# A decoder trunk of two layers in FP32: a third unit of each mixer group by seven products, and two units' low parts summed by DMA

## The chip, the cores and the metric

The kernel runs on one NeuronCore of one Trainium2 chip. The time is the device time of one execution in microseconds; of several runs the median is taken. The engines are TensorE (PE), VectorE (DVE), ScalarE (ACT), GpSimd (POOL) and the queue of SyncE (SP), from which the loads are issued.

## The reference, cut to what matters

Two decoder layers on 256 tokens of width 2048 with FP32 data. Each has a self-attention of 12 heads (a sliding window of 128 in the first layer, one causal block of 256 in the second), 4 heads into 256 memory tokens, an output projection, a layer norm, and a channel mixer with a layer norm behind it:

```
h   = layer_norm(ALPHA * h + mix, g0, b0)
ffn = square(relu(h @ w_up[layer])) @ w_down[layer]      # 2048 -> 8192 -> 2048
h   = layer_norm(ALPHA * h + ffn, g1, b1)
```

The change is in the channel mixer. Everything else of the layers stays as it is.

## The kernel before

Every FP32 operand of a matmul is split into a high part (rounded to a shorter float, tile `whi` for weights) and a low part (what the rounding left, tile `wlo`). A product of two operands is three matmuls into one bank of PSUM: high by high, high by low, low by high (`mm3`, L269 to L273). The split of weights is `split` (L96): ACT writes the high part, DVE subtracts it from the loaded tile `raw` and writes the low part.

The mixer goes through 8192 hidden columns in four chunks of 2048. In a chunk, two up groups compute 1024 hidden columns each, and then two down groups add the chunk's part to 1024 output columns each. A group (`mlp_group`) sums over 2048 inputs in eight units; a unit is a pair of k-tiles of 128 by 1024 columns of weights, 1 MB, loaded by one DMA into one tile `raw`. The 256 tokens are two halves of 128, so a unit is a 2 x 2 by 2 x 2 block product, and there are two ways for it:

- an ordinary unit (`weights`) multiplies every block: 4 banks x 2 k-tiles x 3 matmuls. Its weights are two `whi`/`wlo` pairs of 1024 columns, h0 (B11, B22) and h1 (B12, B21).
- a fast unit takes seven products, by Winograd's form of Strassen's scheme. DVE makes sums of weight blocks in a second tile `t` (`fast_weights`) and sums of activation blocks (`fast_acts`, tiles `sums`, made once and used by all groups with the same activations). Its weights take four `whi`/`wlo` pairs. Three of the products go to banks `P5`, `P6`, `P7` and one to `P1`, which DVE and ACT add up after the last fast unit (`early`); the other three go straight to the group's own banks.

A fixed table, `UP` and `DOWN`, says in which order the units of a group come and how many (those with the lowest numbers) are fast. In both, units 0 and 1 are fast and stand third and fifth. Tiles come from pools with a fixed number of buffers: 7 `whi`, 7 `wlo`, 4 `raw` (shared by loads, `t` and the raw activation sums). An instruction that wants a buffer waits until its last reader is done. On each engine the order of the instructions is written when the kernel is built, by a list scheduler that takes the program's order as its priority.

An up group's result is squared, transposed on PE and split into the next activations `gT`. These transposes (`back`, `transposed`, L443) are put into the stream of the following group at the places of `UHOOKS`: pairs of position in the group and bank. The first use of the activation sums is handed over in the same way, as steps of a generator hung on such places.

In the last chunk of each layer the second down group, and in the second layer the first up group, are plain products (`aform`) and not mixer groups.

Of the kernel before, what the change touches and what calls it, by code (L numbers as in the profile page):

```python
# [9 lines left out]
F32R = mybir.dt.float32r  # L10
I32 = mybir.dt.int32
AF = mybir.ActivationFunctionType
ALU = mybir.AluOpType
AX = mybir.AxisListType

P = 128
# [14 lines left out]
SCALE = float(P) ** -0.5  # L31
SLOPES = [2.0 ** (-8.0 * (i + 1) / HEADS) for i in range(HEADS)]
FAR = -1e33
NRAW = 4
NHI = 7
NLG = 4
HOLD = 13
# [28 lines left out]
NWARM = 2  # L66
FILL = (10, 11, 12, 16)

UP = ((2, 3, 0, 4, 1, 5, 6, 7), 2)
DOWN = ((2, 3, 0, 4, 1, 5, 6, 7), 2)  # L70
UHOOKS = ((0, 3), (1, 0), (1, 2), (1, 3))
WTAIL = ((1, 2), (2, 0), (3, 1), (5, 2), (7, 1), (9, 2))


# [1 line left out]
def trunk(ctx: ExitStack, tc: tile.TileContext, a: dict, out: bass.AP):  # L76
    nc = tc.nc
# [3 lines left out]
    ap_ = ctx.enter_context(tc.tile_pool(name="act", bufs=1))  # L81
# [14 lines left out]
    def split(hi, lo, src):  # L96
        nc.scalar.copy(hi, src)  # L97
        nc.vector.tensor_tensor(lo, src, hi.bitcast(F32), ALU.subtract)  # L98
# [26 lines left out]
    def fast_acts(xs, units):  # L125

        parts = []
        for j in range(0, len(units), 2):  # L130
            n = len(units[j:j + 2])
            x = xs[j // 2][:, :2 * n]
            raw = wp.tile([P, 2, 8, P], F32, name="x_f", tag="raw", bufs=NRAW)
            f = raw[:, 0, :4 * n].rearrange("p (k t) c -> p k (t c)", t=2)
            nc.vector.tensor_tensor(f, x[:, :, 0].bitcast(F32), x[:, :, 1].bitcast(F32), ALU.add)
            a11, a21 = f[:, 0:2 * n:2, :P], f[:, 0:2 * n:2, P:]
            a12, a22 = f[:, 1:2 * n:2, :P], f[:, 1:2 * n:2, P:]
            s = raw[:, 1, :4 * n].rearrange("p (u q) c -> p u q c", q=4)
            nc.vector.scalar_tensor_tensor(s[:, :, 0], a21, -1.0, a22, op0=ALU.mult, op1=ALU.subtract)
            nc.vector.scalar_tensor_tensor(s[:, :, 1], s[:, :, 0], -1.0, a11, op0=ALU.mult, op1=ALU.subtract)  # L140
            nc.vector.tensor_tensor(s[:, :, 2], a11, a21, ALU.subtract)
            nc.vector.tensor_tensor(s[:, :, 3], a12, s[:, :, 1], ALU.subtract)
            parts += [s[:, u] for u in range(n)]
        yield
        for (hi, lo), s in zip(units, parts):
            split(hi, lo, s)
        yield

    def sum_units(n, tags):
        units = []  # L150
        for tag in tags[:n]:
            if tag == "pts":
                units.append([ap_.tile([P, 4, P], F32R, name="sums", tag="pts", bufs=2) for _ in range(2)])
            else:
                t_ = ap_.tile([P, 2, 4, P], F32R, name="sums", tag=tag)
                units.append([t_[:, s] for s in range(2)])
        return units

    def weights(src, parts=1):


        raw = wp.tile([P, 2048], F32, name="raw", tag="raw", bufs=NRAW)
        n = 2048 // parts
        for c in range(0, 2048, n):
            nc.sync.dma_start(raw[:, c:c + n], src[:, c:c + n])
        halves = []
        n = min(n, 1024)
        for s in range(2):
            hi = wp.tile([P, 1024], F32R, name="whi", tag="whi", bufs=NHI)
            lo = wp.tile([P, 1024], F32R, name="wlo", tag="wlo", bufs=NHI)  # L170
            for c in range(0, 1024, n):
                split(hi[:, c:c + n], lo[:, c:c + n], raw[:, s * 1024 + c:s * 1024 + c + n])
            halves.append((hi, lo))
        return halves

# [79 lines left out]
    def mlp_group(src, xts, sums, hooks, early, order, nfast):  # L255

        ps = [ps_mm.tile([P, 512], F32, name="ps_g", tag="mm") for _ in range(4)]
        own = {}  # L260
        seen = {}
        last = {}

        fast = ("P1", 0, 1, "P5", "P7", "P6", 2)
        for u in order:
            for i in range(7 if u < nfast else 4):
                last[fast[i] if u < nfast else i] = (u, i)

        def mm3(bank, x, w, st, en):  # L269
            (xh, xl), (hi, lo) = x, w  # L270
            nc.tensor.matmul(bank, xh, hi, start=st, stop=False)  # L271
            nc.tensor.matmul(bank, xh, lo, start=False, stop=False)  # L272
            nc.tensor.matmul(bank, xl, hi, start=False, stop=en)  # L273

        def tok(k, t):
            return [xts[k // 4][:, k % 4, s, t * P:(t + 1) * P] for s in range(2)]

        left = nfast
        for pos, u in enumerate(order):
            k0, k1 = 2 * u, 2 * u + 1  # L280
            if u < nfast:
                for i in range(4):
                    hooks.get((pos, i), nothing)()
                if not own:
                    for nm in ("P1", "P5", "P6", "P7"):
                        own[nm] = ps_at.tile([P, 512], F32, name=nm, tag="at")
                w = fast_weights(src[u])
                sx = [[s[:, q] for s in sums[u]] for q in range(4)]
                prods = (("P1", tok(k0, 0), "B11"), (0, tok(k1, 0), "B21"), (1, sx[3], "B22"),
                         ("P5", sx[0], "T1"), ("P7", sx[2], "T3"), ("P6", sx[1], "T2"), (2, tok(k1, 1), "T4"))  # L290
                for i, (b, x, wn) in enumerate(prods):
                    mm3(own[b] if b in own else ps[b], x, w[wn], b not in seen, last[b] == (u, i))
                    seen[b] = True
                left -= 1
                if not left:
                    early(own)
                continue
            (h0, l0), (h1, l1) = weights(src[u])
            w = {"B11": (h0[:, :512], l0[:, :512]), "B22": (h0[:, 512:], l0[:, 512:]),
                 "B12": (h1[:, :512], l1[:, :512]), "B21": (h1[:, 512:], l1[:, 512:])}  # L300
            for b in range(4):
                hooks.get((pos, b), nothing)()
                t, n = b // 2, b % 2 + 1
                mm3(ps[b], tok(k0, t), w[f"B1{n}"], b not in seen, False)
                mm3(ps[b], tok(k1, t), w[f"B2{n}"], False, last[b] == (u, b))
                seen[b] = True
        return ps
# [289 lines left out]
    for l in range(LAYERS):  # L597
        more = l + 1 < LAYERS
        wq, wk, wv, wqm = (a[f"{n}{l}"] for n in ("wq", "wk", "wv", "wqm"))
        ps, _ = aform([wv[0, i] for i in range(4)], hT, hooks={6: lambda: next(mem["mk_rest"])})  # L600
        v = evict_v(ps, "v")
# [3 lines left out]
        for g in range(KVH):  # L605
            kt = ap_.tile([P, T], F32, name="kt", tag="kt", bufs=2)
            wform_sum(wk[g], hT, kt, pipe.hooks(*WHOOKS))
            for hd in range(g * GROUP, (g + 1) * GROUP):
                qt = new_q()
# [6 lines left out]
        for m in range(MH):  # L616
            qt = new_q()
# [5 lines left out]
        for nb in range(4):  # L623
            ps, fin = aform([a["wo"][l, nb, i] for i in range(4)], ot, hold=(0 if nb < 3 else 8 if more else HOLD),
                            hooks=pipe.tail() if nb == 0 else {})
# [5 lines left out]
        sum_h = None  # L631
        for c in range(FF // CH):
            gt = new_acts("og", "gT")
            todo = []
            sum_g = sum_units(DOWN[1], ("v", "mk"))
            for v_ in range(CH // 1024):

                hooks = dict(zip(UHOOKS, todo))
                us = [None] * 4
                if c == 0 and v_ == 0 and not more:  # L640
                    for nb in range(2):
                        ps, fin = aform([a["wup_s"][nb, i] for i in range(4)], hT, hold=(16 if nb == 0 else 0))
                        if nb == 0:
                            us[0] = relu2(ps[0])
                            fin()
                            us[2] = relu2(ps[1])
                        else:
                            us[1], us[3] = relu2(ps[0]), relu2(ps[1])
                else:
                    if sum_h is None:  # L650
                        sum_h = sum_units(UP[1], ("sum_h0", "sum_h1", "pts"))
                        steps = fast_acts(hT, sum_h)
                        hooks[0, 0] = hooks[1, 1] = lambda s=steps: next(s)
                    if v_ == 1:
                        steps = fast_acts(gt, sum_g)
                        hooks[5, 0] = hooks[6, 0] = lambda s=steps: next(s)
                    acc = []
                    ps = mlp_group(a["wup"][l, c * (CH // 1024) + v_], hT, sum_h, hooks, sums_up(acc), *UP)
                    for b in range(4):
                        nc.vector.tensor_tensor(acc[b], acc[b], ps[b], ALU.add)  # L660
                        nc.scalar.activation(acc[b], acc[b], AF.Relu)
                        nc.scalar.activation(acc[b], acc[b], AF.Square)
                    us = acc

                def back(b, v_=v_, us=us, gt=gt):
                    transposed(us[b], gt[2 * v_ + b % 2], b // 2, 0)
                todo = [lambda b=b, f=back: f(b) for b in (0, 1, 2, 3)]
# [80 lines left out]
```

## Time and profile before

| | |
|---|---|
| time, median of 3 runs | 2015.75 us (2015.15 to 2016.75) |
| the profiled execution: time | 2016.56 us |
| the profiled execution: span of the core | 2014.4 us |
| mean granted clock of TensorE | 0.997 of full speed |
| TensorE busy | 1994.2 us |
| VectorE busy | 1543.9 us |
| ScalarE busy | 1046.0 us |
| GpSimd busy | 1.2 us |
| moved by DMA | 391.63 MB, 194 GB/s over the span |

The span is one execution as the hardware profiler saw it; the time has some 2 us around it. Busy times say what an engine did, not whether anybody waited for it; matmuls are pipelined, so their records overlap, and the pace is the distance of their starts. Lines (L271) are those of the kernel's listing.

### The profile page before, as it was taken

Reading aid. Unit: us, or ns where it says so; the run is one execution under the profiler, and the core shown is the slowest. Engines: PE = TensorE matmul, PEld = TensorE weight load, DVE = VectorE, ACT = ScalarE, POOL = GpSimd, SP = SyncE. Lnnn points to the kernel's source line nnn. Section 1 sums busy time; section 2 is a strip of 40 time slices with the busy share of each in tenths; the row PEclk is TensorE's granted clock in tenths of the full one; section 3 lists DMA queues with packets and bytes.
Section 4 is the critical chain, followed back from the end, with each engine's and each line's share of the span. In section 5 each row is a group of like instructions: output and inputs, shape, how many; then the busy total and the mean of one; then the engine's idle time right before and its main releaser. Section 6 shows DMA issues by size and latency. Waiting matters only on the chain.

```text
span 2014.4 us, 23998 instructions
## 1 busy us (share of the span) xinstructions
PE 1994.2 (99%) x9326; PEld 1662.3 (83%) x9326; DVE 1543.9 (77%) x1961; ACT 1046.0 (52%) x1361; POOL 1.2 (0%) x8
## 2 busy tenths in 40 slices
PE   9999999999999999999999999999999999999997
PEld 7888888888888888888888888778888888888886
DVE  6566659988787888878785665688878887878885
ACT  6455534654564555466444554346455545654651
POOL 0000000000000000000000000000000000000000
PEclk9999999999999999999999999999999999999999
DMA  9644554555456555456654446445564555555651
GB/s 336 251 160 152 191 185 169 215 203 207 169 186 225 214 177 194 172 188 240 245 225 168 160 160 204 147 146 188 206 216 184 190 186 188 199 218 191 238 209 73
DMA packets 56273, 391.63 MB, mean 194 GB/s; under 512 B 6368, under 2 KB 6368, under 8 KB 9696
## 3 DMA queue, kind: packets, MB, share of 16 engines
q1 hardware_dynamic: 56160, 390.10, 53.7%
q8 instruction: 73, 1.20, 0.2%
q14 instruction: 40, 0.33, 0.0%
HBM read 387.98 MB, written 2.10 MB: 194 GB/s over the span
## 4 chain that ended last, share of the span: by engine, by line
PE 96%; DVE 3%; issue 0%; DMA 0%; ACT 0%; SPq 0%; DVEq 0%
PE ps_g L271 18%; PE ps_g L273 18%; PE ps_g L272 18%; PE ps_w L209 7%; PE ps_a L231 5%; PE ps_a L232 5%; PE ps_a L233 5%; PE ps_w L211 4%; PE P L271 3%; PE P L273 3%; PE P L272 3%; PE pt_h L443 2%; PE ps_m L553 1%; PE ps_m L554 1%; PE ps_m L555 1%; DVE h L436 1%
## 5 line engine op out<-in xcount | busy, mean ns | idle before, releaser
L98 DVE TENSOR_TENSOR wlo<-raw,whi 128x1024 fp32r<-128x1024 f32 (+1 forms) x706 | 818.1, 1174 | 329.7 <-ACT whi L97 325.2
L97 ACT CAST whi<-raw 128x1024 fp32r<-128x1024 f32 (+1 forms) x706 | 697.2, 1014 | 624.5 <-PE ps_g L273 349.7
L271 PE MATMUL ps_g<-whi,hT 128*128 128x512 f32 x780 | 306.7, 393 | 0.0
L273 PE MATMUL ps_g<-whi,hT 128*128 128x512 f32 x780 | 303.8, 390 | 0.0
L272 PE MATMUL ps_g<-wlo,hT 128*128 128x512 f32 x780 | 303.7, 389 | 0.0
L271 PE MATMUL ps_g<-whi,gT 128*128 128x512 f32 x728 | 286.4, 393 | 0.0
L273 PE MATMUL ps_g<-whi,gT 128*128 128x512 f32 x728 | 283.7, 390 | 0.0
L272 PE MATMUL ps_g<-wlo,gT 128*128 128x512 f32 x728 | 283.4, 389 | 0.0
L273 PEld LDWEIGHTS ps_g<-whi,hT 128*128 128x128 f32 x780 | 146.4, 188 | 30.8
L271 PEld LDWEIGHTS ps_g<-whi,hT 128*128 128x128 f32 x780 | 146.5, 188 | 29.4
L272 PEld LDWEIGHTS ps_g<-wlo,hT 128*128 128x128 f32 x780 | 146.6, 188 | 29.3
L273 PEld LDWEIGHTS ps_g<-whi,gT 128*128 128x128 f32 x728 | 136.7, 188 | 28.9
L97 ACT CAST whi<-t 128x1024 fp32r<-128x1024 f32 x116 | 122.0, 1052 | 72.5 <-PE ps_g L273 45.1
L272 PEld LDWEIGHTS ps_g<-wlo,gT 128*128 128x128 f32 x728 | 136.8, 188 | 27.3
L271 PEld LDWEIGHTS ps_g<-whi,gT 128*128 128x128 f32 x728 | 136.7, 188 | 27.2
L98 DVE TENSOR_TENSOR wlo<-t,whi 128x1024 fp32r<-128x1024 f32 x116 | 141.5, 1222 | 20.9 <-ACT whi L97 20.5
L209 PE MATMUL ps_w<-hT,whi 128*128 128x512 f32 x320 | 119.9, 414 | 0.0
L209 PE MATMUL ps_w<-xT,whi 128*128 128x512 f32 x320 | 119.9, 414 | 0.0
L231 PE MATMUL ps_a<-whi,ot 128*128 128x512 f32 x256 | 101.7, 397 | 0.0
L233 PE MATMUL ps_a<-whi,ot 128*128 128x512 f32 x256 | 99.8, 390 | 0.0
L232 PE MATMUL ps_a<-wlo,ot 128*128 128x512 f32 x256 | 99.7, 389 | 0.0
L211 PE MATMUL ps_w<-xT,wlo 128*128 128x256 f32 x320 | 89.9, 281 | 0.0
(170 smaller groups left out, 2832.0 us busy)
## 6 DMA issues: line engine op xcount, KB each, us to landing
raw<-in_wup_dram SPq DMA_DIRECT2D x120, 1024.0 KB, 4.8
raw<-in_wdn_dram SPq DMA_DIRECT2D x112, 1024.0 KB, 4.9
raw<-in_wo_dram SPq DMA_DIRECT2D x32, 1024.0 KB, 4.8
raw<-in_wq_dram SPq DMA_DIRECT2D x24, 1024.0 KB, 4.8
raw<-in_wdn_s_dram SPq DMA_DIRECT2D x16, 1024.0 KB, 4.8
raw<-in_wmk_dram SPq DMA_DIRECT2D x8, 1024.0 KB, 6.2
raw<-in_wv_dram SPq DMA_DIRECT2D x8, 1024.0 KB, 7.3
raw<-in_wk_dram SPq DMA_DIRECT2D x8, 1024.0 KB, 4.9
```

Of the source, the lines that this page charges most:

```text
L97: nc.scalar.copy(hi, src)
L98: nc.vector.tensor_tensor(lo, src, hi.bitcast(F32), ALU.subtract)
L209: nc.tensor.matmul(ps, hi[:, kk:kk + P], x.rearrange("p s t -> p (s t)"), start=(k == 0), stop=False)
L211: nc.tensor.matmul(ps[:, :T], lo[:, kk:kk + P], x[:, 0], start=False, stop=(k == KT - 1))
L231: nc.tensor.matmul(ps[t], xh, hi, start=st, stop=False)
L232: nc.tensor.matmul(ps[t], xh, lo, start=False, stop=False)
L233: nc.tensor.matmul(ps[t], xl, hi, start=False, stop=en)
L271: nc.tensor.matmul(bank, xh, hi, start=st, stop=False)
L272: nc.tensor.matmul(bank, xh, lo, start=False, stop=False)
L273: nc.tensor.matmul(bank, xl, hi, start=False, stop=en)
L436: nc.vector.scalar_tensor_tensor(ht[:, c], ht[:, c], mean, g, op0=ALU.subtract, op1=ALU.mult)
L443: nc.tensor.transpose(pt[:, k], src[:, k * P:(k + 1) * P], ident)
```

## The change

`UP` and `DOWN` now name three fast units, 0, 1 and 2, at the second, fourth and sixth place. The two ordinary units between them, 4 and 5, are listed in `SUMMED`: their low parts are no longer made by DVE. ACT writes the negated high part into `wlo`, a DMA issued from GpSimd adds the loaded weights onto it, and ACT writes the high part. The third unit of activation sums takes buffers of the tags `qt` and `pts`, in quarter tiles, and the splits of the activation sums are made in halves. There are five `raw` buffers. The hooks of the transposes stand earlier, the activation sums of the first layer are made ahead of the first group, and the scratch for GpSimd's DMA descriptors is twice as large.

```diff
-NRAW = 4
+NRAW = 5
...
-UP = ((2, 3, 0, 4, 1, 5, 6, 7), 2)
-DOWN = ((2, 3, 0, 4, 1, 5, 6, 7), 2)
-UHOOKS = ((0, 3), (1, 0), (1, 2), (1, 3))
+UP = ((3, 0, 4, 1, 5, 2, 6, 7), 3)
+DOWN = ((3, 0, 4, 1, 5, 2, 6, 7), 3)
+
+SUMMED = (4, 5)
+UHOOKS = ((0, 1), (0, 2), (0, 3), (1, 0))
...
         for (hi, lo), s in zip(units, parts):
-            split(hi, lo, s)
+            for q in range(2):
+                split(hi[q], lo[q], s[:, 2 * q:2 * q + 2])
...
             if tag == "pts":
-                units.append([ap_.tile([P, 4, P], F32R, name="sums", tag="pts", bufs=2) for _ in range(2)])
+                t_ = [ap_.tile([P, 4, P], F32R, name="sums", tag="pts", bufs=2) for _ in range(2)]
+                units.append([[t[:, :2], t[:, 2:]] for t in t_])
+            elif tag == "qt":
+                t_ = [ap_.tile([P, 2, P], F32R, name="sums", tag="qt", bufs=4) for _ in range(4)]
+                units.append([t_[:2], t_[2:]])
...
-            for c in range(0, 1024, n):
-                split(hi[:, c:c + n], lo[:, c:c + n], raw[:, s * 1024 + c:s * 1024 + c + n])
+            if summed:
+                src_s = raw[:, s * 1024:(s + 1) * 1024]
+                nc.scalar.activation(lo, src_s, AF.Copy, scale=-1.0)
+                nc.gpsimd.dma_start(lo, src_s, accum_op=ALU.add)
+                nc.scalar.copy(hi, src_s)
+            else:
+                for c in range(0, 1024, n):
+                    split(hi[:, c:c + n], lo[:, c:c + n], raw[:, s * 1024 + c:s * 1024 + c + n])
...
-            (h0, l0), (h1, l1) = weights(src[u])
+            (h0, l0), (h1, l1) = weights(src[u], 1, u in SUMMED)
...
-            sum_g = sum_units(DOWN[1], ("v", "mk"))
+            sum_g = sum_units(DOWN[1], ("v", "mk", "pts"))
...
-                        sum_h = sum_units(UP[1], ("sum_h0", "sum_h1", "pts"))
+                        sum_h = sum_units(UP[1], ("sum_h0", "sum_h1", "qt"))
                         steps = fast_acts(hT, sum_h)
-                        hooks[0, 0] = hooks[1, 1] = lambda s=steps: next(s)
+                        if more:
+                            list(steps)
+                        else:
+                            hooks[0, 0] = lambda s=steps: next(s)
+                            hooks[0, 2] = lambda s=steps, f=hooks[0, 2]: (f(), next(s))
...
-    nc = bacc.Bacc("TRN2", target_bir_lowering=False, num_devices=1, dynamic_dma_scratch_size=1024)
+    nc = bacc.Bacc("TRN2", target_bir_lowering=False, num_devices=1, dynamic_dma_scratch_size=2048)
```

## Rows read from the trace of the kernel before

**Rows 1.** The page: busy us (share of span) x instructions; the chain that ended last.

```profile
PE 1994.2 (99%) x9326; PEld 1662.3 (83%) x9326; DVE 1543.9 (77%) x1961; ACT 1046.0 (52%) x1361; POOL 1.2 (0%) x8
...
PE 96%; DVE 3%; issue 0%; DMA 0%; ACT 0%; SPq 0%; DVEq 0%
```

**Rows 2.** PE's waits, whole run: who waited for whom, total us, times, longest.

```profile
PE pt_h L443 <- DVE h L437: 4.2, 2, 2.2
PE ps_m L553 <- ACT whi L97: 2.0, 1, 2.0
```

**Rows 3.** Windows of both layers' mixers: busy us of each engine, clock, DMA.

```profile
core 0: us, PE busy (x) PEld busy (x) DVE busy (x) ACT busy (x) POOL busy (x), PEclk, DMA share, GB/s
...
330.30:1012.00 681.70, 681.70 (x3070) 564.51 (x3069) 564.49 (x630) 377.75 (x444) 0.00 (x0) 1.00 0.56 202
1360.00:1990.00 630.00, 630.00 (x2837) 521.64 (x2836) 512.81 (x574) 338.81 (x397) 0.00 (x0) 1.00 0.54 196
```

**Rows 4.** Groups by line: count, busy us, mean ns, idle before.

```profile
L271 PE MATMUL P<-whi,sums 128*128 128x512 f32 x174 | 67.7, 389 | 0.0
...
L660 DVE TENSOR_TENSOR u_n<-u_n,ps_g 128x512 f32<-128x512 f32 x60 | 41.0, 684 | 11.0 <-PE ps_g L273 9.5
...
L519 DVE SCALAR_TENSOR_TENSOR h<-h,P 128x512 f32<-128x512 f32 x14 | 9.5, 681 | 0.0
```

**Rows 5.** Timeline of PE around one fast unit: start us, us.

```profile
470.64 0.39 PE L273 MATMUL ps_g<-whi,gT 128*128 128x512 f32 x1
...
471.55 0.39 PE L271 MATMUL P<-whi,gT 128*128 128x512 f32 x1
...
476.31 0.39 PE L271 MATMUL ps_g<-whi,gT 128*128 128x512 f32 x1
```

**Rows 6.** Timeline of ACT, the same place; in brackets its idle time before.

```profile
471.12 2.61 ACT L97 CAST whi<-raw 128x1024 fp32r<-128x1024 f32 x3 [3.45 <-PE ps_g L273]
```

**Rows 7.** DVE's groups, shapes kept apart.

```profile
L98 DVE TENSOR_TENSOR wlo<-raw,whi 128x1024 fp32r<-128x1024 f32 x644 | 777.9, 1221 | 323.5 <-ACT whi L97 319.1
L98 DVE TENSOR_TENSOR wlo<-t,whi 128x1024 fp32r<-128x1024 f32 x116 | 141.5, 1222 | 20.9 <-ACT whi L97 20.5
L117 DVE TENSOR_TENSOR t<-raw 128x1024 f32<-128x1024 f32 x58 | 70.8, 1221 | 1.7 <-DMA raw<-in_wdn_dram 0.9 <-DMA raw<-in_wup_dram 0.3
...
L120 DVE TENSOR_TENSOR t<-raw,t 128x512 f32<-128x512 f32 x58 | 40.0, 690 | 1.5
...
L142 DVE TENSOR_TENSOR x_f<-x_f 128x256 f32<-128x256 f32 x10 | 4.3, 425 | 0.3
```

**Rows 8.** ACT's groups, shapes kept apart.

```profile
L97 ACT CAST whi<-raw 128x1024 fp32r<-128x1024 f32 x644 | 659.2, 1052 | 577.6 <-PE ps_g L273 307.8 <-PE ps_a L233 158.5 <-PE ps_w L209 63.0
...
L97 ACT CAST whi<-raw 128x512 fp32r<-128x512 f32 x62 | 38.4, 619 | 46.9 <-PE ps_g L273 41.9 <-DMA raw<-in_wmv_dram 2.3 <-PE ps_a L233 1.7
```

**Rows 9.** DMA: the queue's packets, MB, share; issues with KB, us to landing.

```profile
q1 hardware_dynamic: 56160, 390.10, 53.7%
...
raw<-in_wup_dram SPq DMA_DIRECT2D x120, 1024.0 KB, 4.8
...
raw<-in_wv_dram SPq DMA_DIRECT2D x8, 1024.0 KB, 7.3
...
out_dram<-h SPq DMA_DIRECT2D x8, 256.0 KB, 2.5
ln_row<-in_ln_g_dram SPq DMA_DIRECT2D x2, 512.0 KB, 3.8
```

**Rows 10.** Timeline of PE and of ACT where one group follows another.

```profile
416.58 0.39 PE L271 MATMUL ps_g<-whi,gT 128*128 128x512 f32 x1
...
419.56 0.63 ACT L662 ACTIVATE u_n<-u_n 128x512 f32<-128x512 f32 x1
```

**Rows 11.** Timeline of DVE and PE at the first mixer group of layer 0.

```profile
326.95 1.22 DVE L135 TENSOR_TENSOR x_f<-hT 128x1024 f32<-128x1024 f32 x1
...
342.15 1.23 DVE L98 TENSOR_TENSOR wlo<-t,whi 128x1024 fp32r<-128x1024 f32 x1 [1.19 <-ACT whi L97]
...
330.27 0.48 PE L271 MATMUL ps_g<-whi,hT 128*128 128x512 f32 x1
...
341.25 0.39 PE L271 MATMUL P<-whi,hT 128*128 128x512 f32 x1
```

More of the change, by code (lines that the diff above doesn't have):

```diff
@@ L152, in sum_units, with weights @@
             if tag == "pts":
-                units.append([ap_.tile([P, 4, P], F32R, name="sums", tag="pts", bufs=2) for _ in range(2)])
+                t_ = [ap_.tile([P, 4, P], F32R, name="sums", tag="pts", bufs=2) for _ in range(2)]
[3 more added lines that the diff above has]
+                units.append([t_[:2], t_[2:]])
             else:
                 t_ = ap_.tile([P, 2, 4, P], F32R, name="sums", tag=tag)
-                units.append([t_[:, s] for s in range(2)])
+                units.append([[t_[:, s, :2], t_[:, s, 2:]] for s in range(2)])
         return units
-    def weights(src, parts=1):
+    def weights(src, parts=1, summed=False):
         raw = wp.tile([P, 2048], F32, name="raw", tag="raw", bufs=NRAW)
@@ L287, in mlp_group @@
                 w = fast_weights(src[u])
-                sx = [[s[:, q] for s in sums[u]] for q in range(4)]
+                sx = [[s[q // 2][:, q % 2] for s in sums[u]] for q in range(4)]
                 prods = (("P1", tok(k0, 0), "B11"), (0, tok(k1, 0), "B21"), (1, sx[3], "B22"),
```

## The prediction

> **What bounds the kernel now.** I read the page's busy times and chain first. TensorE (PE) is busy 99% of the span and carries 96% of the chain that ended last [rows 1]. A busy PE can still be a waiting PE, so the waits come next: over the whole run PE's longest named wait is 4.2 us in two places, at the layer norms, and none stands in a mixer stretch [rows 2]. The windows of the mixer say the same: from 330.3 to 1012 and from 1360 to 1990 PE is busy without a gap at a granted clock of 1.00 (the 2.4 GHz level), while VectorE (DVE) is at 82%, ScalarE (ACT) at 55% and the transfers at 0.54 to 0.56 [rows 3]. So time goes by the number of matmuls there, and everything else counts only when it comes late for one.
>
> **What is taken away.** A fast unit has 7 products of 3 matmuls, 21; an ordinary one 4 outputs x 2 k-tiles x 3, 24. In the timeline one fast unit runs from 471.55 to 476.31 [rows 5]: 4.76/21 = 0.2267 us a matmul. The number of groups: 60 evictions with 4 a group are 15 up groups, 14 rows of L519 are 14 down groups, and 174 products P from sums at 3 a fast unit are 58 fast units, two in each of the 29 groups [rows 4]. A third one saves 29 x 3 = 87 matmuls: 87 x 0.2267 = **19.7 us**. With no wait added this is the whole gain.
>
> **What DVE and ACT get.** A fast unit costs DVE one split of 1024 columns from raw, one of 512, two of 1024 from t, one difference of 1024 and two of 512: 1.221 + 0.69 + 2 x 1.222 + 1.221 + 2 x 0.69 = 6.96 us; an ordinary one 2 x 1.221 = 2.44 [rows 7]. The third fast unit adds 4.51 a group. The two summed units take away 4 x 1.221 = 4.88. Net -0.37 a group, -1.5 in a chunk of four groups. The activation sums grow by one unit a chunk: four sums of a half size, about 0.69 + 4 x 0.28 = 1.8 (0.28 is an estimate for 128 columns from the 0.425 of 256), and the splits go from two of 512 columns to six of 256: 6 x 0.425 - 2 x 0.69 = 1.2 [rows 7]. DVE so gains 1.5 us in a chunk; its 82% becomes some 84% of a chunk that is 2.7 us shorter. Without the summed units it would be 4 x 4.51 + 3.0 = 21 us more, over 95%: that is the cover which the accumulating transfers pay for. ACT gets 3 x 1.052 + 0.62 - 2 x 1.052 = 1.67 for the fast unit and 4 x 1.052 = 4.21 for the negated copies, 5.9 a group, some 24 in a chunk [rows 8]: from 55% to about 70%. Both costs lie beside PE; I price them at nothing. If DVE's cover went, each late fast unit would stop PE directly.
>
> **The accumulating transfers.** There are 29 x 2 x 2 = 116 of them, 512 KB each, issued from POOL, whose queue holds nothing else by then. Their place in time is what decides. Seven pairs of hi and lo tiles exist; an ordinary unit holds 2, a fast one 4. While an ordinary unit and the fast one after it are on PE or ready, 6 are taken, so the second half of the summed unit behind them gets its tile only when the ordinary unit drops its own second half. That half is last read three matmuls before the unit ends: by the matmul at 470.64, and ACT starts at 471.12, 0.43 us before the fast unit begins at 471.55 [rows 5, 6]. Before, ACT (1.0) and DVE (1.2) then needed 2.3 us, and the rest was slack. After, ACT writes -hi until about 472.12; then POOL waits, issues, and the sum has to land. The first bank of the summed unit reads the low part of that half with its fifth matmul, at 476.31 + 4 x 0.2267 = 477.22. So a landing has **5.1 us** from ACT's end; what goes beyond it stops PE, 58 times (29 groups x 2 units), and the next summed unit starts from the delayed PE, so nothing is made up. The first half has 10 us and is not at issue. The queued work behind a late sum is only the next sum on POOL, and PE.
>
> No row shows an accumulating transfer or one from POOL. The bounds: 2.5 us (256 KB stored at the end) and 3.8 (512 KB loaded) below; 7.3 above, for 1 MB loads that stood behind others [rows 9]. An accumulating 512 KB reads two operands, so the nearest row is the 1 MB load, 4.8 us [rows 9]. I take 4.8, which is 0.3 short of the limit, and for the loads that cross it (the transfers are busy 0.54 to 0.56 of the time) a mean wait of 0.1 us: 58 x 0.1 = **5.8 us**. The ends are 0 and 58 x 2.2 = 128.
>
> The Trainium skill, "DMA: Bandwidth & Descriptors", section "Anatomy of one DMA", fits a transfer issued by GpSimd with about 2.0 us plus its bytes at 436 GB/s. By it the sum would land in 3.2 us (an estimate from that page) and none would be late; this trace has no GpSimd transfer to compare, and its 1 MB load at 4.8 agrees roughly with the 4.4 of that fit. It says nothing of the second operand.
>
> **The raw tiles.** Four raw buffers become five; one is held longer, until its sum has landed. A group needs 8 loads and 3 t tiles. With four buffers no load is late enough to show at PE [rows 3], and the fifth answers for the longer hold: nothing. All traffic on the queues: 390.1 MB took 53.7% of 2014.4 us [rows 1, 9], so 512 KB is 1.45 us of all engines and, with two operands, up to 2.9; 16 sums a chunk make 23 to 46 us on top of 92, some 68 to 82% of a chunk. No bound by itself.
>
> **Order and hooks.** The transposes of the group before move from 36 to 42 matmuls after their bank ends to 24 for each bank, 5.4 us. Those of the last bank come at the second unit, 24 matmuls after 416.58, at about 422.0 with a little more for the transposes before; its square now ends at 420.19 [rows 10]. Slack 1.8 us: nothing. The gT tiles they fill are first read at the third unit, 5 us later.
>
> At layer 0 the activation sums come before the first weights, and the first fast unit stands second instead of third. Now DVE starts the sums at 326.95 and has the last low part of that fast unit at 343.38, while the group starts at 330.27 and the fast unit at 341.25 [rows 11]. After, the unit would begin 24 matmuls earlier, at 335.8, and wants its last low part 19 matmuls later, at 340.1. DVE's work until then loses one ordinary unit (2.4) and gains 3.0; with the idle time of this stretch (about 2 us) squeezed out it ends near 342.5. I take **2.5 us**, once; ends 0 and 5. In layer 1 two plain products stand before it: nothing.
>
> **The sum.** -19.7 + 5.8 + 2.5 = -11.4. The profiled execution takes 2016.56 (its span 2014.4 and 2.2 around it), so 2005.2 there; the median of the runs shown, 2015.75, lies 0.8 lower: **2004.4 us**, faster by 0.6%. A difference under 0.2%, some 4 us, can't be told from no change.
>
> **Rivals.**
> *The sums are never late.* They land below 5.1 us even beside loads. For it: the 512 KB row of 3.8. Against: loads are in flight half the time [rows 3], and the sum has a second operand to read. 2015.75 - 19.7 + 2.5 = 1998.6, or 1996 if layer 0 hides its start too. This is also what the page's fit above would give. Chance 0.20.
> *The sums are late and PE waits: slower.* Mechanism: the second half of a summed unit can't start before the tile comes free, so a landing above 5.1 us is paid in full, 58 times. It decides from 17.2/58 = 0.30 us on, a landing of 5.4. For it: a load in flight at the same time shares the engines, and the 1 MB row with others ahead is 7.3; two operands at 2.9 us, the 1.9 that the 1 MB row has beyond its packets, and a load's share of 1 give 5.8, a wait of 0.7 and 2015.75 - 17.2 + 58 x 0.7 = 2039. With 1 us it is 2057. Against: both ends of the sum are in SBUF, and the reading of the second operand may overlap. Chance 0.28, half of it above 2038.
> *The fast units' weights are late.* Three fast units each need ACT, DVE sums and DVE again in turn; 0.2 us for each of 87 eats 17.4, no change: about 2016. Against: DVE has a summed unit with no work beside each, 7.0 us in a pair of 10.2, where before a fast and an ordinary unit needed 9.4. Chance 0.10.
> *The forecast*, between 2000 and 2011.7: 0.42.
>
> **How the numbers follow.** Faster by over 0.2%: 0.20 + 0.42 = 0.62; within: 0.10; slower: 0.28. The range goes from 1996 (the whole gain; 0.03 below) to 2038 (half of the slower case beyond, 0.14). The forecast's own range is 2000 to 2012.
>
> **What the profile would show.** Right: 87 matmuls fewer; 116 transfers from POOL of 512 KB landing at about 5 us; PE's waits for them a few us in all; DVE about as busy as now, ACT 24 us more a chunk. Wrong: a row of PE waiting for a DMA on wlo, of tens of us, 58 times; or PE waiting for DVE's wlo from t, or a wait above 5 us at 336 to 342. The step most likely to fail is the 4.8 us.

## The result, and the profile after

The changed kernel takes 2189.97 us (median of 4 runs, 2183.78 to 2193.28) against 2015.45 before: ratio 1.0862, 95% interval 1.0837 to 1.0888. It is 8.6% slower; the forecast was 0.6% faster, and its range ended at 2038.

The page of the changed kernel: busy times, the chain that ended last, the two large DMA queues (packets, MB, share of 16 engines) and the issues of the sums and of one kind of load.

```profile
PE 2040.6 (93%) x9239; PEld 1675.0 (76%) x9239; DVE 1542.8 (70%) x2080; ACT 1193.2 (54%) x1575; POOL 101.9 (5%) x124
...
PE 55%; DMA 15%; issue 9%; DVE 2%; ACT 1%; POOL 1%; POOLq 0%; DVEq 0%; SPq 0%
...
q1 hardware_dynamic: 56160, 390.10, 48.7%
q0 software_dynamic: 16704, 60.82, 14.2%
...
raw<-in_wup_dram SPq DMA_DIRECT2D x120, 1024.0 KB, 5.0
...
wlo<-raw POOLq DMA_DIRECT2D x116, 512.0 KB, 6.4
```

The matmuls fell from 9326 to 9239 [rows 1], the 87 of the forecast. The chain, 96% PE before, is 55% PE and 15% transfers. The span grew by 2191.5 - 2014.4 = 177.1 us. PE's idle time, span less busy, went from 20.2 to 150.9, +130.7; its busy time grew by 46.4 though 19.7 us of matmuls were gone, so the rest ran 66 us slower.

PE's waits over the whole run, the new ones first:

```profile
PE ps_g L287 <- DMA wlo<-raw: 127.3, 48, 6.0
PE pt_h L458 <- DVE h L452: 4.2, 2, 2.2
PE ps_g L286 <- ACT whi L99: 2.5, 2, 2.0
```

All but a few microseconds of the new idle time is PE waiting for a low part, 48 times, up to 6.0 us; no such row stood in [rows 2]. In a summed unit PE's second matmul reads the low part of the first half, its fifth that of the second half. By the sum that ends each wait, 16 waits (58.6 us) are for first halves and 32 (68.7 us) for second halves. One of the first kind, on ACT (the negations are L182, the high parts L184), on POOL and SP, in the chain of waits, and on PE:

```profile
535.24 1.05 ACT L99 CAST whi<-t 128x1024 fp32r<-128x1024 f32 x1 [5.67 <-DVE t L123]
536.20 1.04 ACT L184 CAST whi<-raw 128x1024 fp32r<-128x1024 f32 x1
537.15 2.00 ACT L182 ACTIVATE wlo<-raw 128x1024 fp32r<-128x1024 f32 x2
...
538.56 1.81 POOL L183 DMA_DIRECT2D wlo<-raw  x2 [32.62 <-ACT wlo L182]
...
535.51 0.33 SPq L174 DMA_DIRECT2D raw<-in_wup_dram  x1
537.59 0.33 SPq L107 DMA_DIRECT2D raw<-in_wup_dram  x1
...
538.56 9.62 DMA wlo<-raw
...
541.98 0.39 PE L286 MATMUL ps_g<-whi,hT 128*128 128x512 f32 x1
548.22 0.80 PE L287 MATMUL ps_g<-wlo,hT 128*128 128x512 f32 x1 [5.86 <-DMA wlo<-raw]
```

ACT stands in order behind the cast of the fast unit's block sums, which waits 5.67 us for DVE; only then does it write the negated copies, both halves at once. POOL issues two sums back to back, while two loads of 1 MB issued 3.1 and 1.0 us earlier are on the queues. The sum that PE needs at about 542.2 lands at 548.2. The other kind, two units later in the same group (ACT, the chain, PE):

```profile
554.70 1.06 ACT L182 ACTIVATE wlo<-raw 128x1024 fp32r<-128x1024 f32 x1 [9.35 <-PE ps_g L287]
...
556.12 6.88 DMA wlo<-raw
...
563.05 0.50 PE L287 MATMUL ps_g<-wlo,hT 128*128 128x512 f32 x1 [1.81 <-DMA wlo<-raw]
```

Here ACT waits 9.35 us for a matmul to drop the tile, as the prediction had it, POOL issues 0.36 us after ACT's end, and a landing of 6.88 us is too long for what is left. The windows around the first wait (busy us of each engine, granted clock, DMA share):

```profile
520.00:541.00 21.00, 21.00 (x94) 17.41 (x93) 18.75 (x24) 9.54 (x12) 1.72 (x2) 1.00 0.44 166
541.00:548.00 7.00, 1.37 (x7) 0.79 (x5) 6.23 (x7) 4.35 (x6) 0.86 (x1) 0.81 1.00 218
548.00:552.00 4.00, 3.78 (x9) 2.94 (x10) 0.48 (x1) 0.00 (x0) 0.00 (x0) 0.50 0.88 168
552.00:556.00 4.00, 4.00 (x19) 3.27 (x18) 0.00 (x0) 1.30 (x2) 0.00 (x0) 0.98 0.91 354
```

All 16 DMA engines are busy through the wait (share 1.00). After 6 us of idling PE runs at a granted clock of 0.50, the 1.2 GHz level, and does 9 matmuls in 4 us, then 19 in the next 4. The wait so costs about two microseconds more than its length. The Trainium skill, "TensorE: Matmul & The Clock Gate", section "Part 1: The HAM clock gate", has the slow level as the default that activity lifts; the trace agrees, 1.00 before the wait, 0.50 behind it and 0.98 four microseconds later.

### The profile page after: what moved, and what is told of

The parts are those of the page before. It is cut to its first block, busy times and chain, and to the rows that moved or that the text cites. A ratio compares the mean times of both kernels' runs of the same rounds, so it can differ in the third digit from the quotient of the medians.

```text
span 2191.5 us, 24664 instructions
## 1 busy us (share of the span) xinstructions
PE 2040.6 (93%) x9239; PEld 1675.0 (76%) x9239; DVE 1542.8 (70%) x2080; ACT 1193.2 (54%) x1575; POOL 101.9 (5%) x124
## 3 DMA queue, kind: packets, MB, share of 16 engines
q0 software_dynamic: 16704, 60.82, 14.2%
## 4 chain that ended last, share of the span: by engine, by line
PE 55%; DMA 15%; issue 9%; DVE 2%; ACT 1%; POOL 1%; POOLq 0%; DVEq 0%; SPq 0%
DMA wlo<-raw 14%; PE ps_g L287 11%; PE ps_g L288 10%; PE ps_g L286 10%; PE ps_w L224 3%; PE ps_a L246 3%; PE ps_a L247 3%; PE ps_a L248 3%; PE P L286 2%; PE P L288 2%; PE P L287 2%; PE ps_w L226 2%; PE pt_h L458 1%; POOL wlo L183 1%; DVE wlo L100 1%
## 5 line engine op out<-in xcount | busy, mean ns | idle before, releaser
L100 DVE TENSOR_TENSOR wlo<-raw,whi 128x1024 fp32r<-128x1024 f32 (+1 forms) x590 | 662.0, 1139 | 534.8 <-ACT whi L99 532.5
L99 ACT CAST whi<-raw 128x1024 fp32r<-128x1024 f32 (+1 forms) x590 | 564.9, 985 | 542.5 <-PE ps_g L288 291.8
L286 PE MATMUL ps_g<-whi,hT 128*128 128x512 f32 x690 | 279.0, 409 | 2.5 <-ACT whi L99 2.5
L288 PE MATMUL ps_g<-whi,hT 128*128 128x512 f32 x690 | 278.5, 405 | 0.0
L286 PE MATMUL ps_g<-whi,gT 128*128 128x512 f32 x644 | 257.4, 404 | 0.0
L288 PE MATMUL ps_g<-whi,gT 128*128 128x512 f32 x644 | 256.5, 400 | 0.0
L99 ACT CAST whi<-t 128x1024 fp32r<-128x1024 f32 x174 | 178.6, 1053 | 127.7 <-DVE t L123 94.9
L100 DVE TENSOR_TENSOR wlo<-t,whi 128x1024 fp32r<-128x1024 f32 x174 | 208.1, 1220 | 18.4 <-ACT whi L99 17.6
L183 POOL DMA_DIRECT2D wlo<-raw x116 | 100.7, 870 | 2006.6 <-ACT wlo L182 1852.1
L182 ACT ACTIVATE wlo<-raw 128x1024 fp32r<-128x1024 f32 x116 | 121.3, 1058 | 130.4 <-PE ps_g L287 130.4
L184 ACT CAST whi<-raw 128x1024 fp32r<-128x1024 f32 x116 | 121.0, 1043 | 1.3 <-PE ps_g L288 0.8
L119 DVE TENSOR_TENSOR t<-raw 128x1024 f32<-128x1024 f32 x87 | 106.1, 1220 | 6.6 <-DMA raw<-in_wup_dram 6.4
```

The source lines that it names most:

```text
L119: nc.vector.tensor_tensor(t_[:, 0:2], b[:, 0:2], b[:, 2:3].broadcast_to([P, 2, 512]), ALU.subtract)
L182: nc.scalar.activation(lo, src_s, AF.Copy, scale=-1.0)
L183: nc.gpsimd.dma_start(lo, src_s, accum_op=ALU.add)
L184: nc.scalar.copy(hi, src_s)
```

## The experiments

The theory (L): the loss is PE waiting for sums that land late. The rival (F): ACT and DVE can't feed three fast units, and the sum only shows it because it is the last link. Where the runs left L as the only one, the question was why the sums are late.

**Without the transfers.**

```diff
-                nc.gpsimd.dma_start(lo, src_s, accum_op=ALU.add)
```

> The changed kernel without its 116 accumulating transfers: the low parts of the summed units stay the negated high parts, so these products are not the reference's; everything else (three fast units, the negated copies on ACT, the order, the hooks) stays. Theory L (PE waits only because the sums land late): no wait on a transfer is left, 87 matmuls fewer, 2.5 us at layer 0: 1998 to 2006. Rival F (ACT and DVE no longer feed PE with three fast units; the sums only show it, because they are last in the chain): PE still waits for ACT and DVE at the starts of groups, 2030 to 2120.

Measured: 1999.11 us, ratio 0.992 (0.9904 to 0.9937). Its page:

```profile
PE 1975.7 (99%) x9239; PEld 1646.1 (82%) x9239; DVE 1542.3 (77%) x2080; ACT 1193.0 (60%) x1575; POOL 1.2 (0%) x8
```

The whole loss goes with the transfers, and the time is the one that was worked out without a late sum, 2015.75 - 19.7 + 2.5 = 1998.6. Against this kernel (span 1997.2 us) the changed one has 194.3 us more span, 129.4 of them idle and 64.9 in slower matmuls. Rival F is out. Nor do the transfers slow the engines' own operations: with them ACT's cast of 1024 columns takes 1051 ns and DVE's low part 1222, for 1052 and 1221 in the kernel before [rows 7, 8], and POOL's record of a sum is 0.86 to 1.01 us long.

**All low parts by DVE.**

```diff
-SUMMED = (4, 5)
+SUMMED = ()
```

> The changed kernel with no summed unit: DVE makes all low parts, three fast units stay. Theory L: the loss goes with the transfers; DVE's busy share in the mixer goes to some 95%, so anything from 1998 (DVE just keeps up) to 2040 (it sets the pace in places). Rival F: at least as slow as the changed kernel, 2190 or more, since DVE has 4.9 us a group more to do.

Measured: 2005.02 us, ratio 0.995 (0.9935 to 0.9964). A window in its mixer and its only wait for a low part:

```profile
500.00:700.00 200.00, 200.00 (x897) 164.90 (x896) 185.91 (x220) 110.52 (x136) 0.00 (x0) 1.00 0.54 197
...
PE ps_g L287 <- DVE wlo L100: 0.8, 1, 0.8
```

DVE is busy 185.91 of 200 us, 93%, and PE has no gap. DVE did not need the relief: three fast units alone are 0.5% faster than the kernel before.

**Two fast units, with the sums.** The kernel before with units 4 and 5 summed, five raw buffers and the larger scratch.

```diff
-NRAW = 4
+NRAW = 5
...
-            (h0, l0), (h1, l1) = weights(src[u])
+            (h0, l0), (h1, l1) = weights(src[u], 1, u in (4, 5))
...
```

> The kernel before (two fast units, its order and hooks) with units 4 and 5 summed by accumulating transfers, five raw buffers and the larger scratch. Theory L: the same 116 late sums without the 87 matmuls saved, here each summed unit stands behind a fast one as well: 2150 to 2230. Rival F (three fast units are the load that ACT and DVE can't carry): 2016 to 2060.

Measured: 2292.74 us, ratio 1.1377 (1.136 to 1.1394), over the range expected.

```profile
PE ps_g L278 <- DMA wlo<-raw: 184.7, 74, 4.4
```

Its sums land after 8.9 us in the median, not 6.4, and PE waits 74 times for 184.7 us. The sums do their harm without the third fast unit. Why they do more here stays open.

**The first halves alone.**

```diff
-            if summed:
+            if summed and s == 0:
```

> Only the first half of each summed unit by an accumulating transfer (58 of 116), the second half by ACT and DVE as before. Theory L in its strict form (only the second half has no time, the first half has some 10 us): 2000 to 2015. If the sums are late because of the traffic itself, or because ACT comes late to both halves: PE still waits for sums, about half of the loss, 2060 to 2110.

Measured: 2109.28 us, ratio 1.0468 (1.0441 to 1.0494): the strict form of L falls. The first half does not have 10 us: PE waits 22 times for one, 69.8 us in all. One of its waits (ACT, POOL, the chain, PE):

```profile
476.42 1.05 ACT L99 CAST whi<-t 128x1024 fp32r<-128x1024 f32 x1 [5.72 <-DVE t L123]
477.38 1.05 ACT L184 CAST whi<-raw 128x1024 fp32r<-128x1024 f32 x1
478.32 1.05 ACT L182 ACTIVATE wlo<-raw 128x1024 fp32r<-128x1024 f32 x1
...
479.67 0.86 POOL L183 DMA_DIRECT2D wlo<-raw  x1 [40.69 <-ACT wlo L182]
...
479.67 8.08 DMA wlo<-raw
...
487.80 0.79 PE L287 MATMUL ps_g<-wlo,gT 128*128 128x512 f32 x1 [4.25 <-DMA wlo<-raw]
```

Whether or not its tile is free, ACT comes to it behind the cast that waits 5.72 us for DVE's block sums, and then a single sum takes 8.08 us to land.

**The transfer alone.** Behind the last row of the kernel before, three chains of four transfers of 512 KB, SBUF to SBUF, each waiting for the one before.

```diff
...
+    for _ in range(4):
+        nc.gpsimd.dma_start(lo_s, src, accum_op=ALU.add)
...
+    for _ in range(4):
+        nc.gpsimd.dma_start(lo_c, src)
...
+    for _ in range(4):
+        nc.sync.dma_start(lo_p, src)
```

> The kernel before with twelve transfers of 512 KB, SBUF to SBUF, added behind its last row, each kind a chain in which one waits for the one before, with nothing else on the queues: four accumulating ones from GpSimd, four plain ones from GpSimd into the rounded type, four plain ones from SyncE. If the sum itself is slow: about 4.6 us from issue to landing for the accumulating ones (the shortest in the changed kernel) and 3.3 to 3.8 for the plain ones. If the traffic makes it slow: accumulating ones near 3.5 and hardly longer than plain ones. The result is the reference's; the time is some 40 us longer.

The issues by kind (KB each, median us to landing):

```profile
alone_sum<-alone_src POOLq DMA_DIRECT2D x4, 512.0 KB, 4.4
alone_copy<-alone_src POOLq DMA_DIRECT2D x4, 512.0 KB, 2.8
alone_sp<-alone_src SPq DMA_DIRECT2D x4, 512.0 KB, 2.8
```

With nothing beside it a sum takes 4.4 us, a plain copy 2.8 from either queue. The fit in the Trainium skill, "DMA: Bandwidth & Descriptors", section "Anatomy of one DMA", gives 3.2 (an estimate from that page): GpSimd's plain copy is 0.4 under it, the sum 1.2 over it. The plain copies are below the 3.3 to 3.8 expected. The one run took 2060.18 us, with these chains in it.

**Plain copies for the sums.**

```diff
-                nc.gpsimd.dma_start(lo, src_s, accum_op=ALU.add)
+                nc.gpsimd.dma_start(lo, src_s)
```

> The changed kernel with the 116 transfers as plain copies of the weights over the negated high part, so these low parts are wrong; same bytes written, no second operand read. If the second operand's engine time makes the queues pile up: landings fall to about 4.5 us and the time to 2010 to 2080. If it is the trip through GpSimd's queue that is late, whatever the kind: 2150 to 2190.

Measured: 2123.74 us, ratio 1.0532 (1.0514 to 1.0551), between the two expectations. The queue and the issues:

```profile
q0 software_dynamic: 16704, 60.82, 7.9%
...
wlo<-raw POOLq DMA_DIRECT2D x116, 512.0 KB, 4.5
...
PE ps_g L287 <- DMA wlo<-raw: 77.8, 28, 4.6
```

7.9% of 2123.5 us over 116 is 1.45 us of all engines each; the sum's 14.2% of 2191.5 is 2.68. Against no transfers at all, plain ones cost 125 us and sums 191. What accumulating adds to a copy is a third of the loss; a copy too comes late.

**A quarter of the bytes.** DVE makes the other 768 columns.

```diff
-                nc.scalar.activation(lo, src_s, AF.Copy, scale=-1.0)
-                nc.gpsimd.dma_start(lo, src_s, accum_op=ALU.add)
+                nc.scalar.activation(lo[:, :256], src_s[:, :256], AF.Copy, scale=-1.0)
+                nc.gpsimd.dma_start(lo[:, :256], src_s[:, :256], accum_op=ALU.add)
...
+                nc.vector.tensor_tensor(lo[:, 256:], src_s[:, 256:], hi[:, 256:].bitcast(F32), ALU.subtract)
```

> The transfers sum only the first 256 of 1024 columns of each half; DVE makes the other 768. As many transfers at the same places, a quarter of the bytes. If lateness is bytes on busy queues: 2000 to 2040. If it is a fixed latency of such a transfer against the 5 us that the tiles leave: 2100 to 2180.

Measured: 2061.7 us, ratio 1.0235 (1.0218 to 1.0252), between the two again.

```profile
wlo<-raw POOLq DMA_DIRECT2D x116, 128.0 KB, 6.0
...
PE ps_g L288 <- DMA wlo<-raw: 29.9, 15, 4.3
```

With a quarter of the bytes the median landing hardly falls: 6.0 us, more than a whole sum takes alone, while the shortest takes 2.6. So more than half of the median is not the sum's own. No second half is late any more; all 15 waits for sums are for first halves. PE also waits 14 us for low parts that DVE makes here.

**Half of each load.** The mixer loads 512 KB a unit; the blocks of the other half stand in.

```diff
-        nc.sync.dma_start(raw, src)
+        nc.sync.dma_start(raw[:, :1024], src[:, :1024])
...
-            nc.sync.dma_start(raw[:, c:c + n], src[:, c:c + n])
+            if half:
+                nc.sync.dma_start(raw[:, :1024], src[:, :1024])
...
```

> The changed kernel with half of each mixer weight load left out: 512 KB for 1 MB, and the blocks of the other half stand in for the missing ones, so the mixer's products are not the reference's; all sums, splits and matmuls stay in number, place and size. If the loads beside them make the sums late: landings fall from 6.4 us towards the 4.4 of a sum alone, waits to less than a third, time 2000 to 2060. If sums queue behind each other and behind ACT whatever the loads do: 2130 to 2190.

Measured: 2108.06 us, ratio 1.0459 (1.0444 to 1.0473), between the two.

```profile
wlo<-raw POOLq DMA_DIRECT2D x116, 512.0 KB, 5.1
...
PE ps_g L291 <- DMA wlo<-raw: 60.3, 40, 4.2
```

The landing falls from 6.4 to 5.1 us and PE's waits from 127.3 to 60.3. So the loads beside a sum delay it. But the run moves ACT too: in the changed kernel ACT waits 21 times for DVE's block sums (L123), here once, and the two sums of a unit are issued within 1.2 us of each other twice instead of 14 times. With that the waits for first halves are nearly gone (2, 5.0 us), and 38 waits for second halves stay, 55.4 us of the 68.7. For those the limit of some 5 us is still too short, with landings of 4.4 to 8.9. How much of the gain is lighter queues and how much is an earlier ACT, this run does not part.

**Eight hi and lo tiles.**

```diff
-NRAW = 5
-NHI = 7
+NRAW = 4
+NHI = 8
```

> The changed kernel with eight hi and lo tiles and four raw buffers (five and eight don't fit together). If the start of the second half is held by the number of hi and lo tiles, one more lets it begin earlier, by up to a unit: 2020 to 2110. If it is the traffic, or ACT waiting in order behind the block sums of the fast unit: 2150 to 2220.

Measured: 2176.47 us, ratio 1.0809 (1.0783 to 1.0835). It helps by under 1%. ACT no longer waits for a mixer matmul to drop a tile before a negated copy (22 times, 130.4 us, in the changed kernel), so this hold is gone. But ACT now waits 42 times for DVE's block sums instead of 21, 43 of the 58 pairs of sums are issued within 1.2 us of each other, and they land after 9.0 us in the median; PE still waits 103.4 us for them. One raw buffer fewer may be part of that.

**Units 7 and 3 in place of 4 and 5.**

```diff
-SUMMED = (4, 5)
+SUMMED = (7, 3)
```

> The changed kernel with units 7 and 3 summed in place of 4 and 5: as many transfers, but each of these units stands behind an ordinary unit, not behind a fast one, so its second half gets its tiles some 10 us ahead of its use in place of 5. If it is the lead that decides (a landing of 6 to 11 us against 5): 2000 to 2040. If the sums spoil something else (traffic, ACT's order): 2100 to 2190.

Measured: 2184.81 us, ratio 1.0848 (1.0831 to 1.0864): no better. Units 7 and 3 follow each other, so four sums are issued within 4.6 to 5.8 us in nearly every group and land after 9.2 us in the median. PE's waits:

```profile
PE ps_g L287 <- DMA wlo<-raw: 74.1, 48, 4.5
PE ps_g L286 <- DVE h L465: 21.1, 12, 3.2
PE P L286 <- DVE gT L461: 10.8, 7, 2.0
```

PE waits less for sums, but for DVE's evictions and transposed activations instead, so this run does not single out the lead.

**One unit at a time.** `SUMMED = (4,)`, behind a fast unit, and `SUMMED = (7,)`, behind an ordinary one.

> Three fast units, and only unit 4 (third place, behind a fast unit) summed, both halves: 58 transfers. If the lead of some 5 us is what is too short: PE waits in nearly every group, 2060 to 2110, as with the first halves alone (2109). If it is the number of sums close together: near 2010 to 2030, since two a group leave the queues free.

> As before, but only unit 7 (last place, behind an ordinary unit), 58 transfers too, each with a lead of some 10 us. If the lead decides: hardly a wait, 1999 to 2012. If these sums are late wherever they stand: 2060 to 2110, as for unit 4.

Measured: 2146.37 us, ratio 1.0661 (1.0643 to 1.068), for unit 4, and 2118.44, ratio 1.0513 (1.0496 to 1.0531), for unit 7, both above every range expected. PE's waits with unit 4, then with unit 7:

```profile
PE ps_g L287 <- DMA wlo<-raw: 94.1, 33, 4.6
```

```profile
PE ps_g L287 <- DMA wlo<-raw: 72.4, 43, 6.3
```

Half as many transfers, at either place, keep well over half of the loss. In the kernel with unit 7 (POOL, the chain, PE):

```profile
509.49 1.88 POOL L183 DMA_DIRECT2D wlo<-raw  x2 [40.49 <-DVE h L534]
...
510.49 8.98 DMA wlo<-raw
...
519.52 0.50 PE L287 MATMUL ps_g<-wlo,gT 128*128 128x512 f32 x1 [1.50 <-DMA wlo<-raw]
```

The unit's two sums again leave POOL together, and the second takes 8.98 us. It is issued some 7.5 us before its use, not 10. The longer lead cuts the waits from 94.1 to 72.4 us and does not end them: at neither place is the lead longer than the landing of such a pair.

**The version that the runs point to.** Three fast units, DVE makes all low parts, and the activation sums of layer 0 are back on hooks behind the first weights.

```diff
-SUMMED = (4, 5)
+SUMMED = ()
...
                         if more:
-                            list(steps)
+                            hooks[0, 0] = hooks[0, 2] = lambda s=steps: next(s)
```

> Three fast units, no summed unit, and the activation sums of layer 0 back on hooks of the first unit, behind its weights. If the 2.5 us at layer 0 come from the sums standing ahead of the first weights: 2 to 3 us less than the 2005.0 without that edit. If DVE is the limit there whatever the order: no difference.

Measured: 2001.79 us, ratio 0.9934 (0.9921 to 0.9946). It beats both kernels. Against 2005.02 without the second edit it is 3.2 us less; the two intervals overlap a little, and the traces agree with the sign. In the changed kernel PE waits in the first unit of layer 0, 2.03 and 0.45 us (2.03 and 0.44 without the second edit), since ACT comes to the first weights only behind the activation sums; in this version it waits in the fast unit behind it, 1.27 and 0.22 us. ACT and PE of the changed kernel, then PE of this one:

```profile
331.19 0.43 ACT L99 CAST sums<-x_f 128x256 fp32r<-128x256 f32 x1
331.50 3.48 ACT L99 CAST whi<-raw 128x1024 fp32r<-128x1024 f32 x4
...
332.62 0.49 PE L286 MATMUL ps_g<-whi,hT 128*128 128x512 f32 x1 [2.03 <-ACT whi L99]
333.56 1.09 PE L286 MATMUL ps_g<-whi,hT 128*128 128x512 f32 x2 [0.45 <-ACT whi L99]
```

```profile
341.09 0.50 PE L286 MATMUL P<-whi,sums 128*128 128x512 f32 x1 [1.27 <-ACT whi L99]
342.04 0.50 PE L286 MATMUL ps_g<-whi,hT 128*128 128x512 f32 x1 [0.22 <-ACT whi L99]
```

That is 1.0 us less waiting. The granted clock there differs too: from 330 to 337 us it is 0.79 without the second edit and 1.00 with it, which is 1.5 us of full clock.

## Why the prediction was wrong

**What bounds the kernel; the matmuls taken away.** Right. 9239 matmuls, and without late sums the time was 1999.11 for a worked-out 1998.6.

**The start of layer 0.** Right in size by luck: 2.03 + 0.45 = 2.5 us on PE, for 2.5. The place and the cause were others. The forecast was the fast unit at about 340, waiting for DVE's last low part; PE waited in the first, ordinary unit at 332.6, for ACT, which came to that unit's weights behind the high parts of the activation sums, and not in the fast unit. Behind it the granted clock fell, which had no price.

**What DVE and ACT get.** DVE's busy time hardly moved (1542.8 for 1543.9; 1.5 us a chunk would have been some 11 more), and ACT's grew by 147 us, where 5.9 a group make 171. The conclusion drawn beside it was wrong: without the summed units DVE is at 93% in a stretch of the mixer, near the forecast "over 95%", but PE does not stop. The relief that the sums were to pay for wasn't needed, and the rival in which the fast units' weights come late did not happen.

**The accumulating transfers.** This is the step that failed: "4.8, 0.3 short of the limit", with a mean wait of 0.1 us and 5.8 in all. Against the kernel without transfers they cost 194.3 us of span, 3.35 for each of 58 units. The price of one sum with nothing beside it was fair, 4.4 us measured for the 4.8 taken from a 1 MB load. Three things made it a price of another case:

- *It is not alone.* A sum takes 2.68 us of all 16 engines and a load 2.9, so two sums and two loads are 11 us; the share in the wait shown was 1.00. In 14 of the 29 groups the two sums of unit 4 are issued within 1.1 us of each other; elsewhere the two of a unit are 2.7 to 10.4 us apart, but eight second halves of unit 5 that are issued just behind two loads, 3.5 to 4.1 us after their twin, land after 9.4 to 10.8 us all the same. Landings ran from 4.4 to 11.2 us. The prediction had the mean share of the transfers, 0.54, and from it a wait of 0.1; but the late sums are issued where loads are. The quarter, the half loads and the plain copies, which each take away bytes, each took away a part of the waiting and none all.
- *ACT comes late to it.* The 5.1 us went from a free tile; ACT, in order, was still behind the block sums of the fast unit, 5.7 us in the rows shown, and wrote both halves together. "The first half has 10 us and is not at issue" was wrong: 58.6 of the 127.3 us of waiting are for first halves, and the first halves alone cost 110 us. For 16 of the 32 late second halves the prediction's order holds, a tile that PE drops and a landing that is too long behind it, and there the 0.4 us until POOL issues had no price. Why DVE's block sums stand late there is read from its timeline and was not tried by itself: with the third fast unit sixth, the sums of the P banks fall on the end of the group, among the evictions.
- *A long wait costs more than its length.* There was no term for the granted clock. 64.9 of the 194.3 us are matmuls slower than without the waits. The granted clock is 0.50 in 27 stretches of the changed kernel's trace and in 3 without the transfers; against full clock PE's busy time lost 54.1 us in the former and 3.3 in the latter. So some 51 of the 64.9 us are the clock; the rest stays open.

**Rivals and chances.** The right rival stood there with 0.28: late sums, paid in full, no gain on later ones. It was priced from a landing of 5.8 and a wait of 0.7 or 1 us; the end of the bounds in the text, 2.2 us a unit or 128 in all, is the 127.3 us that PE waited, but by chance: it was meant for second halves alone, which are 68.7 of it. The 64.9 us of slower matmuls come on top. The range should have reached to that bound at least.

**Order, hooks, raw tiles.** As priced, nothing: no wait for a load or a transpose grew beyond a microsecond in the kernel without transfers.

## What to carry to other kernels

Before work is taken from an engine that is 82% busy, run the version in which it keeps that work: 93% was still enough, and the relief cost nearly ten times the gain. A transfer on the path of a unit is priced at its landing with what is issued just before it (its own twin and the loads that the same event sets free), not at the mean share of the queues, and its start from the place in the issuing engine's order, not from the moment its tile comes free. Where PE would wait for several microseconds, add a price for the clock behind the wait: about 2 us in the place shown, some 51 us for all 48 waits.

## What the runs showed of the hardware

- A 512 KB transfer inside SBUF lands after 2.8 us whether GpSimd or SyncE issues it; with accumulation it takes 4.4, and 2.68 us of all 16 engines for 1.45.
- POOL's record of issuing a sum is 0.86 us long.
- Beside 1 MB loads a sum of 128 KB lands after 6.0 us in the median, nearly as late as one of 512 KB (6.4). The shortest of the small ones landed after 2.6 us.
